# One call moved in the Strassen product of a feed-forward block: where the sum W11 + W12 stands in the queue of VectorE

## The chip, the cores and the metric

The kernel runs on one core of a Trainium2 chip. The metric is the device time of one execution in microseconds (us); before the change it is 1196.09 us, the median of three runs (1194.36 to 1196.85).

## The reference

A decoder trunk of two layers for 256 tokens of width 1024, all in float32. Each layer is a SwiGLU feed-forward block (FFN), a token mixer and a second FFN, each with a residual and a LayerNorm:

```python
def _swiglu(x, w1, w3, w2):
    return (jax.nn.silu(x @ w1) * (x @ w3)) @ w2
...
    for l in range(DEPTH):
        h = _swiglu(x, ffn_w1[l, 0], ffn_w3[l, 0], ffn_w2[l, 0])
        x = _layernorm(ALPHA * x + 0.5 * h, ln_g[l, 0], ln_b[l, 0])
        h = _mixer(x, l, w_in[l], ...)
        x = _layernorm(ALPHA * x + h, ln_g[l, 1], ln_b[l, 1])
        h = _swiglu(x, ffn_w1[l, 1], ffn_w3[l, 1], ffn_w2[l, 1])
        x = _layernorm(ALPHA * x + 0.5 * h, ln_g[l, 2], ln_b[l, 2])
```

The hidden width of an FFN is 2816, that is 22 blocks of 128. There are four FFNs in the trunk; the text calls them unit 1 to unit 4 in the order of time. The change lies in the last product of each, `(...) @ w2`.

## The kernel before

**Precision by parts.** TensorE (PE) multiplies in a reduced float32. Each operand is therefore split into a high part and a low part: ScalarE (ACT) writes the high part as a rounded copy (`whi`, lines L195 and L247), VectorE (DVE) writes the rest (`wlo`, lines L197 and L249), and PE adds three products into a bank: high by high, low by high, high by low. Weights come from memory into raw buffers of 128 x 2048 float32 (1 MB, `raw`, four of them), issued by SyncE (SP); each half of such a buffer becomes one pair of parts of 128 x 1024. There are eight buffers for high parts and eight for low ones.

**The product with w2.** `gemm_seven` makes the 256 x 1024 result from 22 blocks of the hidden width. The first eight blocks are done by Strassen's algorithm: the weights of these blocks are four quarters, `w11`, `w12`, `w21`, `w22`, and instead of eight products of quarters there are seven, some of them with sums of weights. The other 14 blocks are multiplied in the plain way; `between()` puts one piece of them (two blocks, 12 matmuls on two banks) after each Strassen product (12 matmuls).

**Where the sums of weights are made.** `r1` is the raw buffer with w11. `r2` is w12, fetched into two buffers of the pool of high parts, called `home`. `plus(r1, r2)` adds r2 to r1 in place on DVE, one instruction for each half (L359). The sum is split by `pieces(r1)` further down and multiplied in `product(bz, sums[0], ...)`. After `plus` has read r2, GpSimd (POOL) lets a DMA add w22 onto it (`gather(r2, w22)`, L353).

**Order.** PE's instructions run in the order in which the program is written. The other engines' instructions are put in order by a scheduler: each fetch of weights raises a counter (`step()`), and what is written after a later fetch has a lower priority. On each engine they run strictly in that order. Within a stretch of an FFN (`line[2]` is set) DVE's splits and sums of weights are also chained to one another: each is scheduled after the one written before it (`behind(line[1])`, `inline(V, ...)`), and the same holds for ACT's splits.

**Other work in the same stretch.** When `gemm_seven` begins, the end of the first product is still under way: the last two column blocks of the hidden layer (`gemm_a2`, whose low parts are multiplied on L302, followed by `r` on ACT L303 and by `silu` on DVE L305 and L925 and ACT L924), two row blocks that are turned by DMA transposes (`planes`, joined again by POOL copies on L229, split by ACT and DVE into `hhi` and `hlo`), the setup of the LayerNorm (`bc`, loads of its gain and bias by POOL, L575; in unit 4 ACT then scales the gain on L594) and the fold of each Strassen product into the residual (`xtok`, L608).

Of the kernel before, what the change touches and what calls it, by code (L numbers as in the profile page):

```python
# [54 lines left out]
def trunk(ctx, tc, x, xT, w13a, w13b, w2, wb, wqk, wu, wg, wgr, wbr, wbrr, wo, gateb, gatebr, sgug, sgub, sguwT, sgubias, lam, diffg,  # L55
# [18 lines left out]
    def name(s):  # L74
        serial[0] += 1
        return f"{s}_{serial[0]}"

    def bank():
        return psum.tile([P, 512], F32, tag="main", name=name("bank"))

    def side_bank():
        return psum.tile([P, 512], F32, tag="side", name=name("sbank"))
# [26 lines left out]
    def step():  # L109
        chunk[0] += 1  # L110
        tc.cur_priority = chunk[0] * STEP
# [12 lines left out]
    def beat(w):  # L124

        clock[0] += w
        for task in list(tasks):
            if task[0] <= clock[0]:
                turn(task)
# [20 lines left out]
    def inline(eng, ins):  # L150
        if line[2]:
            line[eng is V] = ins
        return ins

    def behind(ins):

        return tc.issue_after(ins) if ins is not None else nullcontext()

    def fetch(src, width=CH, raw=None):

        step()
        if raw is None:
            raw = raw_pool.tile([P, CH], F32, tag="raw", name=name("raw"))
        for g in gate:
            g[0] -= 1
        while len(gate) > 1 and gate[1][0] < 0:
            gate.pop(0)
        with behind(gate[0][1] if gate and gate[0][0] < 0 else None):
            if isinstance(raw, list):
                for j, v in enumerate(raw):  # L170
                    loaded[0] = nc.sync.dma_start(v, src[:, j * HC : (j + 1) * HC]).ins
            else:
                loaded[0] = nc.sync.dma_start(raw[:, :width], src).ins
        return raw

    def stream(src, width=CH, sub=HC, lent=(), after=(None, None), pool=()):

        raw = fetch(src, width)  # L180
        out = []
        first = sooner.pop() if sooner else latest
        for o in range(0, width, HC):
            eng = G if o // HC in pool else V
            if o // HC in lent:
                hi, lo = ([act.tile([P, 512], F32R, tag="slot", name=name(n)) for _ in range(2)] for n in ("lhi", "llo"))
                at = [(hi[j], lo[j]) for j in range(2)]
            else:
                hi = hi_pool.tile([P, HC], F32R, tag="hi", name=name("whi"))
                lo = lo_pool.tile([P, HC], F32R, tag="lo", name=name("wlo"))  # L190
                at = [(hi[:, p : p + sub], lo[:, p : p + sub]) for p in range(0, HC, sub)]
            for p, (h, w) in zip(range(0, HC, sub), at):
                r = raw[:, o + p : o + p + sub]
                with behind(first[0]), behind(line[0]):
                    inline(A, A.activation(h, r, AF.Copy).ins)  # L195
                with behind(after[o // HC] or (first[1] if eng is V else None)), behind(line[1] if eng is V else None):
                    low = eng.tensor_tensor(out=w, in0=r, in1=h.bitcast(F32), op=ALU.subtract).ins  # L197
                if eng is V:
                    inline(V, low)
            out.append((hi, lo))  # L200
        return out
# [43 lines left out]
    def split(hi, lo, src, eng=V, after=(None, None)):  # L245
        with behind(after[0]):
            a = A.activation(hi, src, AF.Copy).ins  # L247
        with behind(after[1]):
            return a, eng.tensor_tensor(out=lo, in0=src, in1=hi.bitcast(F32), op=ALU.subtract).ins  # L249
# [94 lines left out]
    def homes(pool, tag):  # L344
        return [pool.tile([P, HC], F32, tag=tag, name=name("home")) for _ in range(2)]

    def halved(v):
        return v if isinstance(v, list) else [v[:, o : o + HC] for o in range(0, CH, HC)]

    def gather(raw, more):  # L350
        step()
        for j, v in enumerate(halved(raw)):
            G.dma_start(v, more[:, j * HC : (j + 1) * HC], accum_op=ALU.add)  # L353
        return raw

    def plus(raw, more):
        for v, m in zip(halved(raw), halved(more)):
            with behind(line[1]):
                inline(V, V.tensor_tensor(out=v, in0=v, in1=m, op=ALU.add).ins)  # L359
        return raw  # L360

    def pieces(raw):
        out = []
        for v in halved(raw):
            hi = hi_pool.tile([P, HC], F32R, tag="hi", name=name("whi"))
            lo = lo_pool.tile([P, HC], F32R, tag="lo", name=name("wlo"))
            for eng, ins in zip((A, V), split(hi, lo, v, after=line[:2])):
                inline(eng, ins)
            out.append((hi, lo))
        return out  # L370

    def product(ps, x, w, start, stop):
        for k in range(4):
            hi, lo = (v[:, k % 2 * 512 : k % 2 * 512 + 512] for v in w[k // 2])
            for n, (y, o) in enumerate(((hi, 0), (lo, 0), (hi, 1))):
                PE.matmul(ps, x[o](k), y, start=start and k == n == 0, stop=stop and k == 3 and n == 2,  # L376
                          skip_group_check=True)
            beat(0.25)

    def gemm_seven(src, xh, xl, sums, ln, done):  # L380

        q = [[bank(), bank()], [side_bank(), bank()]]  # L390
        bx, bz = side_bank(), q[1][0]
        (w11, w21), (w12, w22) = ([s[:, o : o + CH] for o in (0, CH)] for s in src)

        def rest(c):
            for k in range(8, FT, 4):
                nk = min(4, FT - k)
                for j, piece in enumerate(stream(src[c][:, k * 512 : (k + nk) * 512], nk * 512)):
                    yield k + 2 * j, piece

        def rows(t, c, k0, piece, o=0, n=512):  # L400
            for j in range(2):
                k = k0 + j
                hi, lo = (w[:, j * 512 + o : j * 512 + o + n] for w in piece)
                for m, (y, x) in enumerate(((hi, xh), (lo, xh), (hi, xl))):
                    PE.matmul(q[c][t][:, :n] if o == 0 else more[:, :n], x(k, t), y,  # L405
                              start=k == 8 and m == 0 and (c, t) != (1, 0), stop=k == FT - 1 and m == 2, skip_group_check=True)
            beat(n / 1024)

        def block(t, k0):
            return tuple(lambda k, f=f: f(k0 + k, t) for f in (xh, xl))  # L410

        a11, a12, a22 = block(0, 0), block(0, 4), block(1, 4)
        first = rest(0)

        def between():
            k, piece = next(first)
            for t in range(NT):
                rows(t, 0, k, piece)

        r1 = fetch(w11)  # L420
        p1 = pieces(r1)
        r2 = fetch(w12, raw=homes(hi_pool, "hi"))
        plus(r1, r2)
        product(bx, a11, p1, True, False)
        ln.fold(0, 0, bx, ALU.add, True)
        between()
        product(q[0][0], a12, pieces(fetch(w21)), False, False)
        gather(r2, w22)
        r3 = fetch(w22, raw=homes(lo_pool, "lo"))
        between()  # L430
        product(bz, sums[0], pieces(r1), True, False)
        ln.fold(1, 1, bz, ALU.add, True)
        between()
        product(bx, sums[1], pieces(plus(r1, r3)), False, False)
        ln.fold(0, 1, bx, ALU.subtract, True)
        gather(r1, w21)
        between()
        product(bz, sums[3], pieces(r3), False, False)
        between()
        product(bx, sums[2], pieces(r2), False, False)  # L440
        ln.fold(1, 1, bx, ALU.subtract, False)
        between()
        between()
        product(bx, a22, pieces(r1), False, True)
        ln.fold(1, 0, bx, ALU.add, True)
        for t in range(NT):
            done(t, q[0][t], 0, 512)
        held = list(rest(1))
        line[:] = None, None, False
        cuts = ((0, 512),), (((0, 256), (256, 256)) if ln.last else ((0, 512),))  # L450
        for t in range(NT):
            for o, n in cuts[t]:
                more = bank() if o else None
                for k, piece in held:
                    rows(t, 1, k, piece, o, n)
                done(t, (more if o else q[1][t])[:, :n], 512 + o, n)
# [869 lines left out]
```

## Time and profile before

| | us |
|---|---|
| median of 3 runs | 1196.09 |
| lowest, highest | 1194.36, 1196.85 |
| the profiled execution, time | 1197.46 |
| the profiled execution, span from first to last instruction | 1195.7 |
| PE busy | 1185.3 (99%) |
| DVE busy | 1012.0 (85%) |
| ACT busy | 826.2 (69%) |
| POOL busy | 286.1 (24%) |
| mean granted clock of TensorE | 0.998 |

A row of the timeline reads: start, duration, engine, line, operation, output<-inputs, shapes, count, and in brackets the idle time of the engine before it and what ended that idle time. A row "SPq" or "DMA" is an issue or a transfer. The row of the view by windows gives the busy time of each engine in a stretch, the granted clock of PE (PEclk, 1.00 is full) and the busy share of the DMA engines. Times of DVE, ACT and POOL instructions contain a short overlap with their neighbours.

### The profile page before, as it was taken

What the parts mean: (1) busy time and instruction counts of PE and PEld (TensorE: products, weight loads), DVE (VectorE), ACT (ScalarE), POOL (GpSimd) and SP (SyncE); (2) the same over time, 40 slices, a digit from 0 to 9 for tenths busy, and PEclk for the clock granted to TensorE, in tenths of its full rate; (3) what the DMA queues carried; (4) which work ended last, traced back from release to release, by engine and by line L of the source; (5) the groups of instructions that cost most, each with busy time, mean ns of one, the idle gap of its engine ahead of it and who ended that gap; (6) DMA issues with size and microseconds to landing.
All of it is one profiled execution on the core that took longest, in us unless ns stands there. A gap on an engine that the chain in (4) does not pass through costs nothing.

```text
span 1195.7 us, 16657 instructions
## 1 busy us (share of the span) xinstructions
PE 1185.3 (99%) x5771; PEld 994.5 (83%) x5771; DVE 1012.0 (85%) x1558; ACT 826.2 (69%) x1418; POOL 286.1 (24%) x356
## 2 busy tenths in 40 slices
PE   9999999999999999999999999999999999999998
PEld 7888788888888888888888888888888888888787
DVE  6888989788688989889899879888976989988795
ACT  6688558559955677886567876666797556679661
POOL 1111201247420220071020160004464012103200
PEclk9999999999999999999999999999999999999999
DMA  9869975757865658689668699586675764886970
GB/s 351 286 195 275 271 279 203 262 192 216 246 206 186 225 181 272 198 280 262 232 221 264 193 264 293 184 306 213 226 211 190 251 193 155 278 253 217 239 236 36
DMA packets 129797, 276.15 MB, mean 231 GB/s; under 512 B 89089, under 2 KB 90161, under 8 KB 105649
## 3 DMA queue, kind: packets, MB, share of 16 engines
q1 hardware_dynamic: 121968, 248.80, 62.5%
q0 software_dynamic: 7312, 25.76, 9.2%
q8 instruction: 45, 0.74, 0.2%
q10 hardware_dynamic: 432, 0.52, 0.1%
q14 instruction: 40, 0.32, 0.1%
HBM read 249.10 MB, written 1.05 MB: 209 GB/s over the span
## 4 chain that ended last, share of the span: by engine, by line
PE 92%; DVE 4%; DMA 2%; issue 1%; ACT 1%; SPq 0%; DVEq 0%; ACTq 0%
PE bank L283 44%; PE bank L295 14%; PE sbank L376 10%; PE bank L405 9%; PE bank L302 7%; PE sbank L405 3%; PE bank L515 1%; DVE wlo L197 1%; PE sbank L985 1%; DMA home<-in_w 1%; DVE wlo L249 1%; DMA raw<-in_w13b 1%; PE bank L376 1%; PE sbank L1041 1%; PE sbank L1159 1%
## 5 line engine op out<-in xcount | busy, mean ns | idle before, releaser
L197 DVE TENSOR_TENSOR wlo<-raw,whi 128x1024 fp32r<-128x1024 f32 (+1 forms) x374 | 414.7, 1134 | 52.8 <-ACT whi L195 38.0
L195 ACT ACTIVATE whi<-raw 128x1024 fp32r<-128x1024 f32 (+1 forms) x378 | 352.4, 959 | 133.5 <-PE bank L283 43.8
L283 PE MATMUL bank<-whi,x 128*128 128x512 f32 x1224 | 386.5, 390 | 0.0
L283 PEld LDWEIGHTS bank<-whi,x 128*128 128x128 f32 x1224 | 229.8, 188 | 47.7
L283 PE MATMUL bank<-wlo,x 128*128 128x512 f32 x612 | 238.3, 389 | 0.0
L295 PE MATMUL bank<-x,whi 128*128 128x512 f32 x640 | 153.3, 391 | 0.0
L295 PEld LDWEIGHTS bank<-x,whi 128*128 128x128 f32 x640 | 118.2, 188 | 23.8
L283 PEld LDWEIGHTS bank<-wlo,x 128*128 128x128 f32 x612 | 114.9, 188 | 23.4
L249 DVE TENSOR_TENSOR wlo<-raw,whi 128x1024 fp32r<-128x1024 f32 (+1 forms) x96 | 109.3, 1154 | 7.5 <-ACT whi L247 7.2
L247 ACT ACTIVATE whi<-raw 128x1024 fp32r<-128x1024 f32 (+1 forms) x96 | 92.7, 981 | 30.6 <-DVE raw L359 15.4
L302 PEld LDWEIGHTS bank<-x,wlo 128*128 128x128 f32 x640 | 81.4, 191 | 2.9
L229 POOL COPY seven<-seven 128x512 uint16<-128x512 uint16 x16 | 55.9, 3554 | 115.6 <-ACT whi L195 60.8
L302 PE MATMUL bank<-x,wlo 128*128 128x256 f32 x640 | 82.6, 283 | 0.0
L405 PE MATMUL bank<-whi,hhi 128*128 128x512 f32 (+1 forms) x182 | 68.7, 377 | 0.0
L405 PE MATMUL bank<-wlo,hhi 128*128 128x512 f32 (+1 forms) x182 | 68.4, 376 | 0.0
L405 PE MATMUL bank<-whi,hlo 128*128 128x512 f32 (+1 forms) x182 | 68.2, 375 | 0.0
L359 DVE TENSOR_TENSOR raw<-raw,home 128x1024 f32<-128x1024 f32 x32 | 40.4, 1273 | 25.1 <-DMA home<-in_w 22.0
L961 POOL TENSOR_TENSOR swap<-swap,sin_t 128x512 f32<-128x512 f32 x16 | 26.9, 1678 | 103.3 <-DMA swap<-z 77.2
L722 POOL COPY nvia<-ntwo 128x256 uint16<-128x256 uint16 x20 | 9.6, 524 | 155.6 <-DMA ntwo<-nvia 92.5
L303 ACT ACTIVATE r<-bank 128x256 f32<-128x256 f32 x96 | 34.5, 371 | 15.1 <-PE bank L302 15.1
L376 PE MATMUL sbank<-whi,xhs 128*128 128x512 f32 x128 | 42.0, 389 | 0.0
L405 PEld LDWEIGHTS bank<-whi,hhi 128*128 128x128 f32 x182 | 34.6, 190 | 6.2
(283 smaller groups left out, 2155.0 us busy)
## 6 DMA issues: line engine op xcount, KB each, us to landing
raw<-in_w13b SPq DMA_DIRECT2D x68, 1024.0 KB, 5.3
raw<-in_w SPq DMA_DIRECT2D x32, 1024.0 KB, 6.9
raw<-in_wb SPq DMA_DIRECT2D x16, 1024.0 KB, 5.6
raw<-in_wqk SPq DMA_DIRECT2D x16, 1024.0 KB, 6.0
home<-in_w13b SPq DMA_DIRECT2D x16, 512.0 KB, 5.9
raw<-in_w13a SPq DMA_DIRECT2D x8, 1024.0 KB, 4.9
home<-in_w SPq DMA_DIRECT2D x16, 512.0 KB, 6.9
raw<-in_wgr SPq DMA_DIRECT2D x8, 1024.0 KB, 5.2
```

The lines of the kernel that those rows point to most:

```text
L195: inline(A, A.activation(h, r, AF.Copy).ins)
L197: low = eng.tensor_tensor(out=w, in0=r, in1=h.bitcast(F32), op=ALU.subtract).ins
L229: eng.tensor_copy(out=o, in_=i)
L247: a = A.activation(hi, src, AF.Copy).ins
L249: return a, eng.tensor_tensor(out=lo, in0=src, in1=hi.bitcast(F32), op=ALU.subtract).ins
L283: PE.matmul(ps, xx, w, start=start and n == 0, stop=stop and n == 2)
L295: PE.matmul(b[-1], hi[:, k * P : (k + 1) * P], xc(k), start=k == 0, stop=False)
L302: PE.matmul(b[n][:, :T], lo[:, k * P : (k + 1) * P], xc(k)[:, :T], start=False, stop=k == KT - 1)
L303: emptied[0] = A.activation(r[:, s], b[n][:, T:], AF.Copy, scale=scale).ins
L359: inline(V, V.tensor_tensor(out=v, in0=v, in1=m, op=ALU.add).ins)
L376: PE.matmul(ps, x[o](k), y, start=start and k == n == 0, stop=stop and k == 3 and n == 2, skip_group_check=True)
L405: PE.matmul(q[c][t][:, :n] if o == 0 else more[:, :n], x(k, t), y, start=k == 8 and m == 0 and (c, t) != (1, 0), stop=k == FT - 1 and m == ...
```

## The change

The call `plus(r1, r2)` moves down by one product: it is now written behind the first piece of plain rows and behind the split of w21 (the plain block B21 of the algorithm), and in front of the matmuls of that block, not in front of the first product. Nothing is added or left out, and the matmuls of PE stay in their order.

```diff
         r1 = fetch(w11)
         p1 = pieces(r1)
         r2 = fetch(w12, raw=homes(hi_pool, "hi"))
-        plus(r1, r2)
         product(bx, a11, p1, True, False)
         ln.fold(0, 0, bx, ALU.add, True)
         between()
-        product(q[0][0], a12, pieces(fetch(w21)), False, False)
+        p2 = pieces(fetch(w21))
+        plus(r1, r2)
+        product(q[0][0], a12, p2, False, False)
         gather(r2, w22)
```

DVE in unit 4, from the start of `gemm_seven`, before. `raw_11074` is r1, `home_11084` and `home_11085` are the halves of r2; `wlo_11108` and `wlo_11112` are the low parts of the first plain blocks (used by `between()`), `wlo_11132` and `wlo_11136` those of w21, `wlo_11174` the first one of the sum:

```order
L359 TENSOR_TENSOR raw_11074<-raw_11074,home_11084 128x1024
L359 TENSOR_TENSOR raw_11074<-raw_11074,home_11085 128x1024
L197 TENSOR_TENSOR wlo_11108<-raw_11105,whi_11107 128x1024
L305 TENSOR_TENSOR silu_11003<-bank_10947,r_11002 128x256
L197 TENSOR_TENSOR wlo_11112<-raw_11105,whi_11111 128x1024
...
L249 TENSOR_TENSOR wlo_11132<-raw_11129,whi_11131 128x1024
...
L249 TENSOR_TENSOR wlo_11136<-raw_11129,whi_11135 128x1024
...
L249 TENSOR_TENSOR wlo_11174<-raw_11074,whi_11173 128x1024
```

The same place after the change (lines below the edit have a number higher by one). The low parts of the first plain blocks are now `wlo_11106` and `wlo_11110`, those of w21 `wlo_11130` and `wlo_11134`; the inputs `bank` of L305 and `sbank` of L609 are accumulators of PE:

```order
L197 TENSOR_TENSOR wlo_11106<-raw_11103,whi_11105 128x1024
L197 TENSOR_TENSOR wlo_11110<-raw_11103,whi_11109 128x1024
L249 TENSOR_TENSOR wlo_11130<-raw_11127,whi_11129 128x1024
L305 TENSOR_TENSOR silu_11003<-bank_10947,r_11002 128x256
L305 TENSOR_TENSOR silu_11003<-bank_10960,r_11002 128x256
L249 TENSOR_TENSOR wlo_11134<-raw_11127,whi_11133 128x1024
...
L359 TENSOR_TENSOR raw_11074<-raw_11074,home_11084 128x1024
L609 TENSOR_SCALAR xtok_143<-xtok_143,sbank_11073 128x512
...
L359 TENSOR_TENSOR raw_11074<-raw_11074,home_11085 128x1024
L575 COPY bc_11057<-silu_11029 128x1
...
L249 TENSOR_TENSOR wlo_11174<-raw_11074,whi_11173 128x1024
```

The two sums went from the front of the stretch to a place behind the four low parts, and the low parts of the sum follow closely behind them.

ACT in unit 2 where the high parts of the sum stand, before. `raw_5378` is r1, `planes` are the turned row blocks that POOL joins, `silu` comes from DVE:

```order
L247 ACTIVATE hhi_4308<-silu_5311 128x256
L247 ACTIVATE whi_5477<-raw_5378 128x1024
L247 ACTIVATE hhi_4306<-planes_5180 128x512
L247 ACTIVATE hhi_4308<-silu_5337 128x256
L247 ACTIVATE whi_5481<-raw_5378 128x1024
L247 ACTIVATE hhi_4307<-planes_5196 128x512
```

And after:

```order
L247 ACTIVATE hhi_4308<-silu_5311 128x256
L925 ACTIVATE silu_5337<-silu_5337 128x256
L247 ACTIVATE hhi_4306<-planes_5180 128x512
L247 ACTIVATE hhi_4307<-planes_5196 128x512
L247 ACTIVATE hhi_4308<-silu_5337 128x256
L247 ACTIVATE whi_5477<-raw_5378 128x1024
L247 ACTIVATE whi_5481<-raw_5378 128x1024
```

Both high parts of the sum now stand behind both splits of `planes`. On POOL the two DMAs of `gather(r2, w22)` move behind the last copies of `planes`: in units 2 and 3 they stood on either side of them.

## The prediction

> **What bounds the kernel now.** The page comes first: its first section gives each engine's busy time.
>
> ```profile
> PE 1185.3 (99%) x5771; PEld 994.5 (83%) x5771; DVE 1012.0 (85%) x1558; ACT 826.2 (69%) x1418; POOL 286.1 (24%) x356
> ```
>
> PE is busy 99% of the span. The change takes nothing from PE and keeps its order, so it can only win what PE loses by waiting, or add to that. Hence the view of waits, first of PE alone, then of all engines.
>
> ```profile
> PE bank L376 <- DVE wlo L249: 3.9, 3, 1.9
> ...
> PE sbank L376 <- DVE wlo L249: 0.6, 1, 0.6
> ```
>
> ```profile
> DVE raw L359 <- DMA home<-in_w: 22.0, 8, 3.9
> ```
>
> PE waits four times in the Strassen products of w2, for a low part that DVE makes: three times into a `bank` (the plain block w21), once into an `sbank`. And DVE idles 22.0 us in front of the eight sums r1+r2, until `home`, the w12 halves, has landed. The change moves exactly these eight instructions. The timeline of PE shows the waits; unit 1:
>
> ```profile
> 129.60 0.39 PE L376 MATMUL bank<-whi,hhi 128*128 128x512 f32 x1
> 130.95 0.50 PE L376 MATMUL bank<-wlo,hhi 128*128 128x512 f32 x1 [0.95 <-DVE wlo L249]
> ...
> 132.21 0.40 PE L376 MATMUL bank<-whi,hhi 128*128 128x512 f32 x1
> 133.62 0.49 PE L376 MATMUL bank<-wlo,hhi 128*128 128x512 f32 x1 [1.01 <-DVE wlo L249]
> ...
> 137.62 0.39 PE L376 MATMUL sbank<-whi,hhi 128*128 128x512 f32 x1
> 137.84 0.39 PE L376 MATMUL sbank<-wlo,hhi 128*128 128x512 f32 x1
> ...
> 144.06 0.50 PE L376 MATMUL sbank<-wlo,sum 128*128 128x512 f32 x1 [0.62 <-DVE wlo L249]
> ```
>
> Undisturbed matmuls start 0.22 to 0.23 us apart (137.62, 137.84). So the waits for w21 cost 1.35-0.23 = 1.12 and 1.41-0.23 = 1.18 us. Unit 4 has the third one, and something behind it:
>
> ```profile
> 1133.46 0.40 PE L376 MATMUL bank<-whi,hhi 128*128 128x512 f32 x1
> 1135.74 0.50 PE L376 MATMUL bank<-wlo,hhi 128*128 128x512 f32 x1 [1.89 <-DVE wlo L249]
> ...
> 1138.39 0.63 PE L405 MATMUL bank<-whi,hlo 128*128 128x512 f32 x1
> ...
> 1139.96 0.39 PE L405 MATMUL bank<-whi,hhi 128*128 128x512 f32 x1
> ...
> 1147.01 0.39 PE L376 MATMUL sbank<-wlo,sum 128*128 128x512 f32 x1
> ```
>
> ```profile
> 1105.00:1145.00 40.00, 38.04 (x175) 31.29 (x174) 30.90 (x41) 26.57 (x42) 9.02 (x11) 0.96 0.92 266
> ```
>
> The wait costs 2.28-0.23 = 2.05 us. After it matmuls take 0.63 us in place of 0.39, and the row by windows has a granted clock of 0.96: PE ran slowly for some 3.5 us. From 1135.74 to 1139.96 there are eleven starts, which at 0.227 us are 2.50; they took 4.22, so the slow clock cost 1.7 us.
>
> The timeline of DVE shows why w21 is late (first unit 4, then unit 1):
>
> ```profile
> 1120.64 1.23 DVE L359 TENSOR_TENSOR raw<-raw,home 128x1024 f32<-128x1024 f32 x1 [3.36 <-DMA home<-in_w]
> 1125.76 1.23 DVE L359 TENSOR_TENSOR raw<-raw,home 128x1024 f32<-128x1024 f32 x1 [3.90 <-DMA home<-in_w]
> 1126.90 1.22 DVE L197 TENSOR_TENSOR wlo<-raw,whi 128x1024 fp32r<-128x1024 f32 x1
> 1128.04 0.42 DVE L305 TENSOR_TENSOR silu<-bank,r 128x256 f32<-128x256 f32 x1
> ...
> 1134.47 1.22 DVE L249 TENSOR_TENSOR wlo<-raw,whi 128x1024 fp32r<-128x1024 f32 x1
> ...
> 1140.87 2.35 DVE L359 TENSOR_TENSOR raw<-raw,home 128x1024 f32<-128x1024 f32 x2
> 1144.21 1.23 DVE L249 TENSOR_TENSOR wlo<-raw,whi 128x1024 fp32r<-128x1024 f32 x1 [0.99 <-ACT whi L247]
> ```
>
> ```profile
> 119.88 1.22 DVE L359 TENSOR_TENSOR raw<-raw,home 128x1024 f32<-128x1024 f32 x1 [3.35 <-DMA home<-in_w]
> 123.23 1.22 DVE L359 TENSOR_TENSOR raw<-raw,home 128x1024 f32<-128x1024 f32 x1 [2.13 <-DMA home<-in_w]
> ...
> 135.34 1.22 DVE L249 TENSOR_TENSOR wlo<-raw,whi 128x1024 fp32r<-128x1024 f32 x1
> ...
> 142.79 1.22 DVE L249 TENSOR_TENSOR wlo<-raw,whi 128x1024 fp32r<-128x1024 f32 x1
> ```
>
> DVE stands 7.3 us in unit 4 and 5.5 us in unit 1 with the sums at its head. Behind them are the low parts of the plain blocks and of w21, whose high parts are done:
>
> ```profile
> 1120.82 1.07 ACT L247 ACTIVATE whi<-raw 128x1024 fp32r<-128x1024 f32 x1 [0.75 <-PE bank L295]
> 1122.63 1.06 ACT L247 ACTIVATE whi<-raw 128x1024 fp32r<-128x1024 f32 x1 [0.75 <-PE bank L295]
> ...
> 1142.17 1.06 ACT L594 ACTIVATE bc<-bc 128x1024 f32<-128x1024 f32 x1 [4.37 <-DVE raw L359]
> ```
>
> w21's second high part was ready at 1123.7, its low part began at 1134.47. From the second sum on DVE has no pause up to 142.79 in unit 1 and to 1143.22 in unit 4: a late start is carried through the whole queue.
>
> **The change part by part.** *Sums out of the front.* An instruction of 128x1024 takes 1.14 us from start to start (1126.90 to 1128.04). While `home` is still on its way DVE now makes the two low parts of the plain blocks (2.28 us), and in the best case one of w21 and two `silu` (1.14+2x0.33 = 1.8 us). Those of w21 may have to wait for buffers that L302 is reading:
>
> ```profile
> 1122.43 4.00 PE L302 MATMUL bank<-x,wlo 128*128 128x256 f32 x32
> ```
>
> L302 frees four buffers between 1123.4 and 1126.4. Even the last of these leaves w21's second low part, by my estimate from these rows, at about 1130, against its use at 1135.5 less the waits. So all three waits for w21 go: 1.12+1.18 in unit 1, 2.05 in unit 4, with the slow clock 1.7.
>
> *The sums, now later.* The first of them (1.14 us) falls into the busy stretch, where before it lay in the idle one. Against the old queue DVE is ahead by 2.28-1.14 = 1.1 us at least and 1.1+1.8 = 2.9 at most. What is late next is read at two places. The sum r1+r2: in unit 1 its first low part ended at 136.56 (row 135.34), now at 133.7 to 135.5; PE wants it at 137.84-2.30 = 135.54. No wait, at the lower bound just so. The sum r1+r3: in unit 1 its low part ended at 144.0, where PE waited 0.62 to 0.77; now at 141.1 to 142.9, and PE, 2.30 us earlier, wants it at 144.06-0.77-2.30 = 141.0. There the earlier PE runs into DVE again, and what unit 1 keeps is DVE's lead: 1.1 to 2.9 us. I take the middle, 2.0.
>
> In unit 4 the same low part began at 1144.21 after ACT, which had idled up to L594, the scaling of `bc`. The row names DVE, but L594 needs only the transfer of `bc`, which POOL issued 5.9 us before:
>
> ```profile
> 1136.32 0.55 POOL L575 DMA_DIRECT2D bc<-in_lng  x1 [7.96 <-ACT whi L247]
> ```
>
> The tiny copy that lets POOL issue it stands behind the second sum on DVE, and POOL now issues the two `gather` DMAs of r2 right in front of it. With DVE's lead of 1.1 to 2.9 us the low part ends at 1142.5 to 1144.3 in place of 1145.4; PE wants it at 1147.01-2.05-1.7 = 1143.3. So 0 to 1.0 us is lost again; I take 0.4. Unit 4 keeps 3.75-0.4 = 3.4, between 2.7 and 3.8.
>
> *Units 2 and 3.* The view of waits has none of them, so nothing is to be won: 0, between -0.2 and +0.5.
>
> *Other queues.* SP gets raw and low buffers back some 5 us sooner and fetches sooner; `gather(r2, w22)` comes 5 to 8 us later, but r2 is multiplied only three products behind the sum. I put both at 0.
>
> *The sum.* 2.0+3.4 = 5.4 us, so the profiled execution, 1197.46, would take 1192.1. Its time lies 1.4 us above the median of the runs, and the slow clock is the term that may be missing in other executions; I count half of it for the median: 5.4-0.9 = 4.5, so 1196.09-4.5 = **1191.6 us**. With all bounds the gain is 1.1+2.7-1.7 = 2.1 to 2.9+3.8+0.4 = 7.1.
>
> **The rivals.** *The wait only moves (0.14).* PE comes earlier and meets r1+r2 or r1+r3 late in more places: DVE's lead of 1.1 us is all that is won in units 1 and 4, and units 2 and 3 lose 0.5 each. 1196.1-2.2+1.0 = 1194.9. For it: DVE is busy without a pause up to r1+r3. Against it: in unit 4 ACT and DVE idle at that place.
>
> *POOL starves and the kernel is slower (0.07).* ACT now splits both `planes` ahead of the sum's high parts, and `planes` need copies of POOL. These ran while DVE idled; other copies of the kind did not:
>
> ```profile
> 1121.72 1.44 POOL L229 COPY planes<-planes 128x512 uint16<-128x512 uint16 x2 [7.26 <-DMA planes<-planes]
> ...
> 1123.63 1.75 POOL L229 COPY planes<-planes 128x512 uint16<-128x512 uint16 x2
> ```
>
> ```profile
> 508.67 16.88 POOL L229 COPY seven<-seven 128x512 uint16<-128x512 uint16 x2 [27.05 <-ACT whi L195]
> ```
>
> Now DVE works in that gap. If the last two copies took 16.9 us from 1123.6, they would end at 1140.5, and with a high and a low part (1.06+1.14) the sum would be there at 1142.7, where PE wants it at some 1137.8: 4.9 us, and 1.7 for the clock. In four units that is 26, less the 6.1 of the waits gone: 1216. It decides from copies of 12 us on. Against it: four L305 and a fold, which read a bank of PE, stand among DVE's instructions there, and DVE still pauses for L302's buffers. The Trainium skill says this in "SBUF — State Buffer", section "Who interferes with whom": a DVE instruction with two SBUF inputs locks out a GpSimd instruction that reads SBUF, one with at most one SBUF input does not. The 16.88 us beside the 1.44 agree with it.
>
> *The slow clock stays (0.09).* It may come from something else than the wait; then the gain is 1.7 less on the profiled execution: 1193.3. For the wait as its cause: of PE's waits in the view the longest (1.9) is the one with the slow stretch right behind it. The Trainium skill, "TensorE: Matmul & The Clock Gate", Part 1, has the clock halved after an idle window of about 3.4 us. By that rule 1.89 us would not be enough, and the slow stretch would stay; here the row right behind the wait speaks against it.
>
> **How the numbers follow.** Forecast 0.70, the rivals 0.14, 0.07 and 0.09. A measurement of this kernel can tell 0.2% (2.4 us) from no change: 1193.7 to 1198.5 is the same. Forecast and slow clock are faster (0.79, of which 0.01 goes to the same for the lowest gains), the moved wait is the same (0.15 with it), starving is slower (0.07). 0.78, 0.15, 0.07. The range goes from 1196.1-7.1 = 1189.0 to 1195.0, which takes in the moved wait.
>
> **What would show it.** Right: no bracket before w21's `wlo` matmuls; DVE's L359 (r1+r2) without idle time for `home`; a granted clock of 1.00 near 1135; perhaps 0.5 to 1.5 us before the r1+r3 products. Wrong: PE waiting at r1+r2 (137.6 and 1141.3 before), POOL copies of `planes` over 5 us, or ACT idle before the splits of `planes`.

## The result, and the profile after

The changed kernel takes 1192.52 us (median of 9 runs, 1190.89 to 1194.45), the kernel before 1195.61 us (9 runs, 1193.90 to 1197.15). The ratio is 0.9975, interval 0.9965 to 0.9986: 3.1 us faster, between 1.7 and 4.2. The forecast was 4.5 us and 1191.6. In the profiled executions the span goes from 1195.7 to 1191.8 us. First the page's busy times, then the view of waits of PE, both of the changed kernel (lines behind the edit count one more than in the kernel before):

```profile
PE 1182.0 (99%) x5771; PEld 993.3 (83%) x5771; DVE 1012.0 (85%) x1558; ACT 827.5 (69%) x1418; POOL 291.3 (24%) x356
```

```profile
PE sbank L376 <- DVE wlo L249: 1.8, 2, 1.0
PE bank L516 <- ACT whi L247: 1.4, 2, 0.8
...
PE sbank L376 <- ACT whi L247: 0.8, 1, 0.8
```

The row `PE bank L376`, the waits for w21, is gone. What is left in w2 stands at `sbank`, the products of sums, and one of these waits is now for ACT. The 1.4 us at L516 is the start of the program, before anything that was changed. PE's timeline, unit 1 and then unit 4:

```profile
131.48 0.39 PE L376 MATMUL bank<-whi,hhi 128*128 128x512 f32 x1
131.70 0.39 PE L376 MATMUL bank<-wlo,hhi 128*128 128x512 f32 x1
...
141.00 0.39 PE L376 MATMUL sbank<-whi,sum 128*128 128x512 f32 x1
142.40 0.50 PE L376 MATMUL sbank<-wlo,sum 128*128 128x512 f32 x1 [1.02 <-DVE wlo L249]
```

```profile
1130.86 0.39 PE L376 MATMUL bank<-whi,hhi 128*128 128x512 f32 x1
1131.08 0.39 PE L376 MATMUL bank<-wlo,hhi 128*128 128x512 f32 x1
...
1140.15 0.39 PE L405 MATMUL bank<-whi,hlo 128*128 128x512 f32 x1
1141.33 0.49 PE L376 MATMUL sbank<-whi,sum 128*128 128x512 f32 x1 [0.79 <-ACT whi L247]
1142.59 0.50 PE L376 MATMUL sbank<-wlo,sum 128*128 128x512 f32 x1 [0.76 <-DVE wlo L249]
```

In w21 the low part follows the high part after 0.22 us in both units. At r1+r3 unit 1 still waits, 1.40-0.23 = 1.17 us there, and unit 4, which had no wait at that place before, now loses 1.18-0.23 = 0.95 and 1.26-0.23 = 1.03 us. The row by windows over unit 4 has the granted clock at 1.00, 0.96 before:

```profile
1105.00:1145.00 40.00, 38.37 (x182) 31.56 (x181) 31.13 (x41) 27.39 (x41) 15.78 (x13) 1.00 0.91 253
```

The timelines of DVE, ACT and POOL in unit 4 show why r1+r3 is late:

```profile
1126.20 1.21 DVE L359 TENSOR_TENSOR raw<-raw,home 128x1024 f32<-128x1024 f32 x1
...
1128.87 1.21 DVE L359 TENSOR_TENSOR raw<-raw,home 128x1024 f32<-128x1024 f32 x1
...
1135.27 2.35 DVE L359 TENSOR_TENSOR raw<-raw,home 128x1024 f32<-128x1024 f32 x2
1141.31 1.22 DVE L249 TENSOR_TENSOR wlo<-raw,whi 128x1024 fp32r<-128x1024 f32 x1 [3.69 <-ACT whi L247]
```

```profile
1139.27 1.06 ACT L595 ACTIVATE bc<-bc 128x1024 f32<-128x1024 f32 x1 [6.13 <-DMA bc<-in_lng]
1140.23 1.99 ACT L247 ACTIVATE whi<-raw 128x1024 fp32r<-128x1024 f32 x2
```

```profile
1127.94 0.85 POOL L353 DMA_DIRECT2D home<-in_w  x1 [4.51 <-PE sbank L376]
1130.61 0.84 POOL L353 DMA_DIRECT2D home<-in_w  x1 [1.82 <-DVE bc L575]
1131.15 0.86 POOL L576 DMA_DIRECT2D bc<-in_lng  x1
```

The sums r1+r2 no longer wait for `home` (no bracket), and DVE has r1+r3 done at 1137.6. But ACT has stood for 6.13 us at the scaling of `bc`, whose transfer POOL issued at 1131.15, behind the two gathers, and which ACT could read 8.1 us later (5.85 before: 1136.32 to 1142.17). Only then ACT makes the high parts, and DVE waits 3.69 us for them.

### The profile page after: what moved, and what is told of

The parts are those of the page before. It is cut to its first block, busy times and chain, and to the rows that moved or that the text cites. A ratio compares the mean times of both kernels' runs of the same rounds, so it can differ in the third digit from the quotient of the medians.

```text
span 1191.8 us, 16673 instructions
## 1 busy us (share of the span) xinstructions
PE 1182.0 (99%) x5771; PEld 993.3 (83%) x5771; DVE 1012.0 (85%) x1558; ACT 827.5 (69%) x1418; POOL 291.3 (24%) x356
## 3 DMA queue, kind: packets, MB, share of 16 engines
HBM read 249.10 MB, written 1.05 MB: 210 GB/s over the span
## 4 chain that ended last, share of the span: by engine, by line
PE 96%; DVE 2%; DMA 1%; issue 1%; SPq 0%; ACT 0%; ACTq 0%; DVEq 0%
PE bank L283 46%; PE bank L295 15%; PE sbank L376 11%; PE bank L405 9%; PE bank L302 7%; PE sbank L405 3%; PE bank L516 1%; PE sbank L986 1%; DMA raw<-in_w13b 1%; PE bank L376 1%; PE sbank L1042 1%; PE sbank L1160 1%; DVE wlo L249 1%; PE sbank L1040 0%; DVE raw L359 0%
## 5 line engine op out<-in xcount | busy, mean ns | idle before, releaser
L376 PE MATMUL sbank<-whi,xhs 128*128 128x512 f32 x128 | 42.0, 389 | 0.0
L405 PEld LDWEIGHTS bank<-whi,hlo 128*128 128x128 f32 x182 | 34.3, 188 | 6.1
```

## The experiments

**Where the time is lost, by unit.** The half changes come first. `late` stands for the new place of the sum; `unit` counts the calls of `gemm_seven`.

```python
+        late = unit[0] in (1, 4)      # u14;  u23: (2, 3)
+        if not late:
+            plus(r1, r2)
...
+        p2 = pieces(fetch(w21))
+        if late:
+            plus(r1, r2)
```

u14: 

> The new order of the sum in units 1 and 4 only, the old one in units 2 and 3. Theory (all of the gain is PE's waits for w21's low parts, and those exist in units 1 and 4 alone): the whole gain, -3.1 us against the kernel before (between -2 and -4), no PE wait for w21, and the r1+r3 waits of about 1.2 us in unit 1 and 2.2 us in unit 4 as in the changed kernel. Rival (the gain is spread over all units, for instance by home and raw buffers that come free earlier): about half, -1.5 us.

u23: 

> The new order in units 2 and 3 only. Theory: no change within +-1 us of the kernel before; PE's three waits for w21 are there again (1.1, 1.2 and about 2 us over the normal 0.23), and behind unit 4's a stretch of matmuls of 0.63 us in place of 0.39 if the slow clock comes from the wait. Rival (gain spread over all units): -1.5 us. Rival for the clock (it has another cause): the unit 4 wait is there and no slow stretch follows.

Measured: u14 1194.16 us, ratio 0.9988 (0.9979 to 0.9997); u23 1194.88, ratio 0.9995 (0.9986 to 1.0004); the kernel before in the same hour 1195.73. One of the eleven runs of u14 took 2414.78 us, twice the others, and is left out of its ratio. So u14 gives 1.6 us, half of what the theory said, and u23 0.9 us or nothing. Neither theory nor rival is settled by times of this size. The trace of u23 surprised more: unit 4 in the old order had hardly a wait for w21, and no slow clock there; its slow stretch lies at the start of the program (last section).

A ledger of the traces says more than the times do. Every trace holds the same 5771 rows of PE in the same order. I took best_again (below), which has no wait at L376 at all, as the ruler and compared start by start: what the difference of the starts grows by across a stretch is what a kernel loses there more than the ruler. In us:

| profiled execution | first 20 us | unit 1: w21 | unit 1: r1+r3 | unit 2 | unit 3 | unit 4: w21 | unit 4: r1+r3 |
|---|---|---|---|---|---|---|---|
| before | -0.30 | 2.57 | 1.12 | 0.06 | 0.31 | 4.17 | 0.00 |
| before_again | 0.21 | 2.18 | 1.05 | 0.92 | 0.33 | 0.43 | 1.17 |
| u23 | 1.77 | 2.25 | 1.06 | 0.00 | 0.00 | 0.53 | 0.47 |
| after | 0.21 | 0.00 | 1.32 | 0.00 | 0.00 | 0.00 | 2.51 |
| after_again | 0.26 | 0.00 | 1.17 | 0.00 | 0.00 | 0.00 | 1.27 |
| u14 | 0.20 | 0.00 | 1.25 | 0.13 | 0.25 | 0.00 | 1.75 |
| sum_self | -0.27 | 0.00 | 0.31 | 0.00 | 0.00 | 0.00 | 0.00 |
| bc_later | 0.27 | 0.00 | 1.31 | 0.00 | 0.00 | 0.00 | 0.00 |
| best | -0.77 | 0.00 | 0.09 | 0.00 | 0.00 | 0.00 | 0.00 |
| best_old23 | 0.49 | 0.00 | 0.06 | 0.42 | 0.13 | 0.00 | 0.00 |
| best_old23_again | -0.16 | 0.00 | -0.01 | 0.07 | 0.69 | 0.00 | 0.00 |
| best_old4 | 0.53 | 0.00 | 0.11 | 0.00 | 0.00 | 0.84 | 0.00 |

Unit 1's loss at w21 in the old order is steady, 2.2 to 2.6 us. Unit 4's is 4.17 in the execution on which the forecast was built, and 0.43, 0.53 and 0.84 in three others.

**Is it the idle time for `home`?** The sum stays at the head of DVE's queue, but its second operand is r1 itself, so that it waits for no transfer (r2 is left out of the sum, and the output is another one).

```python
-        plus(r1, r2)
+        plus(r1, r1)
```

> The kernel before, with the sum in its old place at the head of DVE's queue, but adding r1 to itself: the second operand r2 is left out, so that nothing waits for home (the output is another one). Theory (what delays w21 is DVE's idle time for home, not the place of the sum as such): no PE wait for w21 in units 1 and 4, a gain like the change's, -2 to -5 us. Rival (the two sums are simply too much work ahead of the low parts): the waits for w21 stay, less than 1 us is gained.

Measured: 1189.80 us, ratio 0.9950 (0.9938 to 0.9963), 5.9 us faster than before. DVE's timeline of unit 1 in this kernel, and the whole answer of its view of PE's waits:

```profile
116.49 3.38 DVE L359 TENSOR_TENSOR raw<-raw 128x1024 f32<-128x1024 f32 x2
```

```profile
PE bank L515 <- ACT whi L247: 1.2, 1, 1.2
PE sbank L527 <- DVE warm L523: 1.0, 1, 1.0
PE sbank L658 <- ACT minus L656: 0.7, 1, 0.7
```

The sums run at 116.5 us, where in the kernel before DVE idled, and no wait at L376 is left. So not the place of the sum but the idle time for `home` held w21 up. The 5.9 us are not the price of w21 alone: POOL also issues the transfer of `bc` in unit 4 earlier (1128.78, 1136.32 before), and there is no loss at r1+r3 there either. The changed kernel gets half of the 5.9 us.

**What is late next in unit 4.** The scaling of `bc` goes behind the high parts of r1+r3 on ACT; nothing else moves.

```python
-                A.activation(self.g, self.g, AF.Copy, scale=-0.5)
...
-        product(bx, sums[1], pieces(plus(r1, r3)), False, False)
+        p3 = pieces(plus(r1, r3))
+        if ln.last:
+            with behind(line[0]):
+                A.activation(ln.g, ln.g, AF.Copy, scale=-0.5)
+        product(bx, sums[1], p3, False, False)
```

> The changed kernel, with ACT's scaling of bc in unit 4 (L595) queued behind the high parts of r1+r3 rather than in front of them. Theory (unit 4 loses 2.2 us at r1+r3 because ACT stands 6.1 us at L595 for the transfer of bc): the two waits at r1+r3 of unit 4 go, 1.5 to 2.2 us are gained on the changed kernel, -4.6 to -5.3 us against the kernel before. Rival (the sums r1+r3 or their low parts would be late by DVE's own work): the waits stay, now named for DVE, and the time is the changed kernel's, -3.1 us.

Measured: 1190.60 us, ratio 0.9957 (0.9944 to 0.9969): 5.1 us faster than before, the changed kernel's 3.1 and 2.0 more. PE's timeline of unit 4 in bc_later, at the place where the changed kernel waited twice, and ACT's:

```profile
1140.31 0.39 PE L376 MATMUL sbank<-whi,sum 128*128 128x512 f32 x1
1140.53 0.39 PE L376 MATMUL sbank<-wlo,sum 128*128 128x512 f32 x1
```

```profile
1138.61 1.04 ACT L438 ACTIVATE bc<-bc 128x1024 f32<-128x1024 f32 x1
```

No bracket: the theory holds, DVE's own queue was not late there.

**What is late next in unit 1.** On top of bc_later, the setup of small tables (gbh, lam, dgs) begins 8 beats later (the program counts PE's work in beats and starts side work by them). In unit 1 of the changed kernel it stood on DVE just ahead of r1+r3. This kernel is best.

```python
-        yield 22
+        yield 30
```

> The changed kernel with bc scaled later (as in bc_later) and with the small setup of unit 1 (gbh, lam, dgs) begun at 30 beats rather than 22, so that it lies behind r1+r3 on DVE and its exponent behind the high parts on ACT. Theory (unit 1's last wait at r1+r3, 1.2 us, comes from DVE's queue, which holds about 1 us of setup in front of the sum): about 1.0 us less than bc_later, 1189.6 us, no PE wait at L376 anywhere. Rival (ACT's high part is what is late there): 0 to 0.3 us less than bc_later.

Measured: 1189.43 us, ratio 0.9940 (0.9928 to 0.9953). DVE's timeline of unit 1 in best, and PE's:

```profile
133.82 2.35 DVE L197 TENSOR_TENSOR wlo<-raw,whi 128x1024 fp32r<-128x1024 f32 x2
136.09 2.35 DVE L359 TENSOR_TENSOR raw<-raw,home 128x1024 f32<-128x1024 f32 x2
```

```profile
140.01 0.39 PE L376 MATMUL sbank<-whi,sum 128*128 128x512 f32 x1
140.24 0.49 PE L376 MATMUL sbank<-wlo,sum 128*128 128x512 f32 x1
```

The sums now follow the low parts directly, and the wait of 1.17 us is gone. The ledger gives 1.31-0.09 = 1.22 us for it, near the 1.0 of the theory; the medians of the two differ by 1.2 us too, but were taken on different chips. This is the fastest version of all, 0.6% under the kernel before (0.5% in its second load, below).

**The old order put back, unit by unit, in best.**

best_old23: 

> The same kernel (best) with the old order of the sum in units 2 and 3. Theory (units 2 and 3 had next to nothing to lose): 0.3 us slower than best, since the trace of before shows three short waits at r1+r3 in unit 3, 0.3 us in all. Rival (units 2 and 3 do give a part of the gain, as the -1.6 and -0.9 us of the two half changes would say): 1 to 1.5 us slower than best.

best_old4: 

> The same kernel (best) with the old order of the sum in unit 4 alone. Theory (unit 4's wait is for a transfer, home, whose landing differs from run to run): 0.5 to 2.5 us slower than best, and in a run with the longest wait up to 4.2 us, by the slow clock; the runs spread over 2 us or more where those of best lie within 1 us. Rival (the wait is the same in each run, 2.3 us, with the slow clock 4.1): 4 us slower, with a spread as small as that of best.

Measured: best_old23 1190.87 us (ratio 0.9953), 1.44 us over best, as the rival had it; best_old4 1190.18 (0.9946), 0.75 us over best. The runs of best_old4 spread over 1.4 us, those of best over 1.1: neither what theory nor rival said of the spread, though the size agrees with the theory. The traces disagree with the 1.44: units 2 and 3 lose 0.42+0.13 us, while the first 20 us differ by 0.49+0.77 = 1.26. The views of PE's waits, best_old23 and then best, show that start:

```profile
PE bank L527 <- ACT whi L247: 2.4, 2, 1.3
```

```profile
PE bank L520 <- ACT whi L247: 0.6, 2, 0.3
```

**The same kernels loaded anew**, to see what a load has of its own.

best_again: 

> best, unchanged, loaded anew. Theory (loads differ): within 1 us of its first load (0.9940 of the kernel before), no PE wait at L376. Rival (no such offset): within 0.3 us of it.

best_old23_again: 

> best with the old order in units 2 and 3, unchanged, loaded anew. Theory (the 1.4 us by which it was slower lay in the first 10 us of its load, where the profiles differ by 1.3 us, and not in units 2 and 3): 0.2 to 0.6 us slower than best_again, once the difference of the two starts is taken off. Rival (units 2 and 3 do give 1 to 1.5 us): 1.4 us slower again, with a start as in best_again.

before_again: 

> The kernel before, unchanged, loaded as a kernel of its own beside the kernel before. Theory (a load has a time of its own, by the first weights, for which PE waited 0.2 to 2.4 us in the profiles so far): the two equal kernels may differ by up to 1 us in the median. Rival (no such offset): within 0.4 us. Its profile is also a second look at unit 4: theory (the 2.05 us wait with the slow clock was a rare one): a wait of 0.5 to 1.5 us and no slow clock; rival: 2 us and the slow clock again.

after_again: 

> The changed kernel, unchanged, loaded anew. Theory (unit 1 gives 2.3 us, unit 3 0.3; in unit 4 the waits at r1+r3 that come cost about as much as the usual wait for w21 that goes): 2 to 3 us faster than the kernel before, and again about 1.2 us lost at r1+r3 in unit 1 and 1.8 to 2.5 in unit 4. Rival (unit 4 gives 3.4 us, as forecast): 4 us or more.

| kernel | us | runs | ratio to before |
|---|---|---|---|
| best_again | 1189.65 | 1189.28 to 1190.25 | 0.9948 (0.9935 to 0.9960) |
| best_old23_again | 1189.97 | 1189.26 to 1190.44 | 0.9948 (0.9935 to 0.9962) |
| after_again | 1192.78 | 1190.98 to 1193.15 | 0.9972 (0.9961 to 0.9984) |
| before_again | 1196.36 | 1194.60 to 1199.89 | 1.0005 (0.9996 to 1.0014) |
| before | 1196.09 | 1193.86 to 1197.37 | |

best_old23 is now 0.32 us behind best, not 1.44: the rival's number came with that load and its start. The second loads of best, of the kernel before and of the changed kernel differ from the first by only 0.2 to 0.3 us, so an offset of a whole microsecond is not the rule (best was on another chip the first time, where the kernel before took 1196.81 us). What sets the wait at the start was not pursued.

before_again shows another execution of the kernel before. Its waits of PE (the two rows of `bank` are w21 in unit 1), its timeline of DVE in unit 4, and PE's there:

```profile
PE sbank L376 <- DVE wlo L249: 1.4, 3, 0.6
...
PE bank L376 <- DVE bc L574: 1.0, 1, 1.0
...
PE bank L376 <- DVE wlo L249: 0.5, 1, 0.5
```

```profile
1123.63 2.02 DVE L359 TENSOR_TENSOR raw<-raw,home 128x1024 f32<-128x1024 f32 x1 [2.55 <-DMA home<-in_w]
```

```profile
1133.92 0.39 PE L376 MATMUL bank<-whi,hhi 128*128 128x512 f32 x1
1134.40 0.50 PE L376 MATMUL bank<-wlo,hhi 128*128 128x512 f32 x1
```

The second sum of unit 4 starts at 1123.63 rather than 1125.76, though PE itself comes a little later than in before; w21's low part is then late by 0.48-0.23 = 0.25 us and not by 2.05. The wait depends on when a transfer lands, and this differs from execution to execution. after_again repeats the gain, 3.3 us; its loss at r1+r3 in unit 4, 1.27 us, is below the 1.8 to 2.5 expected.

**The clock.** In best, PE is stopped on purpose ahead of w21 in unit 4:

```python
+            PE.matmul(q[1][1][:, :P], warm, warm, start=True, stop=True, skip_group_check=True)
+            for _ in range(5):
+                A.activation(warm, q[1][1][:, :P], AF.Copy)
+            PE.matmul(q[1][1][:, :P], warm, warm, start=True, stop=True, skip_group_check=True)
```

> The same kernel (best) with a wait put into PE's stream on purpose in unit 4, just ahead of w21's product: a matmul into a bank not yet in use, five small copies of it by ACT, and a matmul that needs the last of them. By the rows of ACT there it stops PE for 2 to 4 us. Theory (it is PE's wait that brings the slow clock: a window of 3.41 us in which PE idles more than half makes the next one slow): a 3.41 us stretch at a granted clock of 0.5 follows in most runs, and the time grows by the wait and 1.7 us. Rival (the slow stretch of before had another cause, or needs a whole idle window): the time grows by the wait alone and the clock stays at 1.0.

Measured: 1194.79 us, 5.36 over best. PE's timeline of clk5, then the row by windows of two stretches of 3.41 us, columns as in the prediction (PE busy first, the granted clock third from the end):

```profile
1128.08 0.23 PE L429 MATMUL bank<-warm 128*128 128x128 bf16 x1
1131.52 0.23 PE L432 MATMUL bank<-warm 128*128 128x128 bf16 x1 [3.21 <-ACT warm L431]
...
1132.90 0.63 PE L376 MATMUL bank<-whi,hlo 128*128 128x512 f32 x1
```

```profile
1129.23:1132.64 3.41, 1.12 (x6) 0.96 (x7) 3.41 (x5) 2.20 (x5) 1.88 (x3) 1.00 0.98 177
1132.64:1136.05 3.41, 3.41 (x10) 2.63 (x9) 1.53 (x3) 1.06 (x1) 0.00 (x0) 0.50 1.02 306
```

The stop is followed by 3.41 us at half clock; by the ruler it costs 5.2 us, 3.5 for the stop with its two matmuls and 1.7 behind it. Half a clock over 3.41 us takes 0.0014 off the mean clock of a run: all eleven runs of clk5 show 0.999 or 0.997, four of five of best 1.000. So a stop of PE does bring the slow clock, and the third rival falls for the profiled execution. Of the 52 runs of the kernel before in these comparisons 39 have a mean clock of 1.000, so the slow stretch of its profile was in 13 of them at most. The changed kernel has 1.000 in 9 of 15 runs (after and after_again), no larger a share, so the runs do not show that it is rid of slow stretches. The mean clock does not say where they lie: u14's profile has 0.999 from the last 2.3 us of the program alone, in which PE does nothing.

## Why the prediction was right or wrong

**Right: unit 1.** 2.0 us forecast, 2.57-(1.32-1.12) = 2.37 in the first pair of traces, 2.18-(1.17-1.05) = 2.06 in the second. The rest wait was foreseen at r1+r3; that it would be the setup in DVE's queue was not.

**Right: the cause, the quiet places.** Idle time for `home` was what held w21 up (sum_self). No wait came at r1+r2, and ACT was not idle before the splits of `planes`. POOL did not starve; its row of unit 4 in the changed kernel has four copies in 3.79 us, 0.95 each, where the rival needed 12:

```profile
1119.64 3.79 POOL L229 COPY planes<-planes 128x512 uint16<-128x512 uint16 x4 [6.75 <-ACT whi L247]
```

**Wrong: unit 4, the cost at r1+r3.** 0 to 1.0 us was forecast, 0.4 taken, and 2.51 measured. The step that failed is that DVE's lead of 1.1 to 2.9 us would bring the low part forward: the chain there begins with the transfer of `bc`, and its new place behind the two gathers was named in the prediction and given no price. PE's first matmul of `gemm_seven` in unit 4 already comes 2.2 us earlier (1126.27 to 1124.03). Counted from there the issue of `bc` came 2.9 us earlier (1136.32 to 1131.15, less 2.2), but its landing and the low part only 0.7 (1142.17 to 1139.27 and 1144.21 to 1141.31), while PE came 4.2 us earlier (1146.78 to 1140.38, where it would start without the wait). That the gathers made the transfer longer is argued, not shown, though the traces go with it: from issue to landing it took 5.6 to 6.3 us in the four with the old order in unit 4 (before, before_again, u23, best_old4), 6.6 to 8.1 in the nine with the new one, and 4.4 in sum_self, whose gathers run some 10 us ahead of it. No run moved the gathers alone. What is shown is that this transfer, through ACT, is all of the wait (bc_later). So unit 4 gave 4.17-2.51 = 1.66 in the profiled pair, not 3.4.

**Wrong: unit 4, how often.** The 2.05 us wait with its slow clock was one execution's. The forecast took the whole wait into the median and half of the clock's 1.7, that is 3.4-0.9 = 2.5 us. In the second pair unit 4 gives 0.43-(1.27-1.17) = 0.33: here the wait has only moved, to r1+r3, as the first rival said, but through ACT and the transfer of `bc`, not because DVE was busy. The third rival's time should have been near 1192.4: its 1193.3 takes the 1.7 us of the clock off a gain from which 0.9 of them were gone already, and 5.4-1.7 is 3.7. That is near the measured 1192.52, so the time alone does not tell this rival from the forecast; clk5 does, for the execution profiled.

**Wrong, the other way: units 2 and 3.** 0 was forecast (up to 0.5), since the view of waits has no row of them. Their losses come in pieces too short for it, or in other executions: 0.06+0.31 in before, 0.92+0.33 in before_again, and none in the changed kernel. So they give 0.4 to 1.25 us. The forecast's bounds have no term for its -0.2 below and 0.4 for its +0.5 above; with both they are 1.9 and 7.2, not 2.1 and 7.1.

**The sum.** First pair: 2.37+1.66+0.37 = 4.4, less 0.5 for a slower start. Second pair: 2.06+0.33+1.25 = 3.6, against 3.3 between the two spans (1193.9 and 1190.6), the rest at the start and the end. That the time came out within 0.9 us is in part luck: the kernel before measured 0.5 us less than when the forecast was made, so the gain was missed by 1.4 us (3.1 for 4.5), and it was not missed by more because unit 4 was taken too high and units 2 and 3 too low. How much each unit gives on average is open: there are two to four traces of each, and u14 and u23 were not sharp enough.

## What to carry to other kernels

An instruction that waits for a transfer at the head of an in-order queue delays everything behind it that is ready: queue the ready work first, and then look for the next instruction of the same kind (here `bc` on ACT), since the engine that waits comes earlier and meets it. A wait for a transfer seen in one profile is one draw; before it is priced, look at a second execution, and at the spread of the runs (3.5 us in 16 runs of the kernel before, 1.0 us in five of best_again, without such waits). A view of waits that has no row for a stage does not show that the stage loses nothing: compare the starts of the same instructions with a trace that has no waits.

## What the runs showed of the hardware

The clock halved after a stretch in which PE was not fully idle. In the kernel before, the row by windows of the 3.41 us ahead of the slow stretch, and of the slow stretch:

```profile
1132.97:1136.38 3.41, 1.52 (x7) 0.92 (x6) 3.29 (x7) 3.41 (x6) 0.06 (x1) 1.00 0.95 372
1136.38:1139.79 3.41, 3.41 (x10) 2.63 (x9) 3.41 (x5) 1.42 (x2) 1.04 (x2) 0.50 1.01 392
```

PE's longest wait there was 1.89 us, so no 3.41 us were idle throughout. The start of u23, where PE waited 1.79 us for the first weights, shows the same:

```profile
7.88:11.30 3.42, 1.63 (x8) 1.08 (x7) 1.31 (x3) 1.47 (x3) 0.00 (x0) 1.00 1.01 383
11.30:14.72 3.42, 3.42 (x10) 2.65 (x9) 2.25 (x5) 2.49 (x5) 0.00 (x0) 0.50 1.06 412
```

PE was busy for 1.52 of 3.41 us in the kernel before, for 1.12 in clk5 and for 1.63 in u23, and the next 3.41 us ran at 0.50 in all three. The Trainium skill, "TensorE: Matmul & The Clock Gate", Part 1, gives a free-running window of 3413 ns, with which the length agrees, and the slow clock after at least one idle window; here a stretch that was 48% busy was enough. A stretch of the same length around the waits of unit 1 in the kernel before, 129.45 to 132.86, was busy for 2.21 us (65%), and the clock stayed at 1.00. Where between these the limit lies was not tried.
